# A list scheduler's view of PSUM banks and of weight loads, in a one-core hybrid diffusion step

## The chip, the core and the metric

The kernel runs on one core of one Trainium2 chip. Its time is the device time of one execution in microseconds (us); the median of three runs is the metric. The engines are TensorE (PE in the profile, with its weight loads as PEld), VectorE (DVE), ScalarE (ACT), GpSimd (POOL) and SyncE (SP), which issues the DMA transfers.

## The reference

One inference step of a two-layer hybrid backbone (DEPTH is 2) over 128 prompt tokens and 512 latent tokens, in fp32, with D_MODEL 1024 and D_FF 2816. Cut to what matters:

```python
def _token_mixer(h, lw, ctx):
    (z, xbc, dt_raw, rq, rk, rv, rg, aq, ak, av, mcq, mckv) = jnp.split(h @ lw['w_in'], split_at, axis=-1)
    xbc = jax.nn.silu(_dwconv_centred(xbc, lw['ssd_conv_w'], lw['ssd_conv_b']))
    ...
    y, ssd_f, ssd_b = _bidir_scan(ch, bh * dt[:, :, 0, :, None], ...)          # SSD, 8 heads
    o_ssd = _rmsnorm(y.reshape(bsz, L, SSD_INNER) * jax.nn.silu(z), lw['ssd_norm_w'])
    o, ret_f, ret_b = _bidir_scan(rq, rk, rk, rv, la_f, la_b, ...)             # retention, 4 heads
    o_ret = (_head_layernorm(o)... * lw['ret_gn_w'] * jax.nn.silu(rg))
    o_att = _attention(q_att, keys, vals, ATT_HEAD_DIM ** -0.5)...             # grouped-query, 8 heads
    o_mla = _attention(q_m, k_m, v_m, (MLA_NOPE + MLA_ROPE) ** -0.5)...        # latent attention, 8 heads
    g = jax.nn.sigmoid((h @ lw['w_merge'] + lw['b_merge']).astype(f32))
    merged = (g[:, :, 0] * (o_ssd @ lw['w_br_ssd']) + g[:, :, 1] * (o_ret @ lw['w_br_ret'])
              + g[:, :, 2] * (o_att @ lw['w_br_att']) + g[:, :, 3] * (o_mla @ lw['w_br_mla']))
    return merged @ lw['w_out'], cache

def _trunk_layer(x, mod, lw, ctx):      # mod = silu(cond) @ w_mod + b_mod
    h = _rmsnorm(x, lw['g_pre_mix']) * (1.0 + sc_a) + sh_a
    x = x + g_a * _rmsnorm(_token_mixer(h, lw, ctx), lw['g_post_mix'])
    h = _rmsnorm(x, lw['g_pre_ffn']) * (1.0 + sc_f) + sh_f
    return x + g_f * _rmsnorm(_conv_ffn(h, lw), lw['g_post_ffn'])
```

## The kernel before

**Products.** Activations lie feature-major, 128 features by 640 tokens a tile, in two halves of 320 tokens. Every linear layer takes each weight as a high part and a low part, and each activation likewise (`ah0` to `ah7` and `al0` to `al7` are the eight tiles of the normed input). One 128x128 weight block and one half of the tokens make three matmuls of 320 columns into a PSUM bank `lin`: high weight by `ah`, high weight by `al`, low weight by `ah`. The weights come in blocks of 512 columns: `weights()` has SP load `wr` (256 KB), ACT copy it to `wh` (the high part), and DVE subtract to `wl` (the low part, called the split below). There are four buffers of `wr`, three of `wh` and three of `wl`.

**Order.** The kernel's Python doesn't issue instructions. A `Recorder` keeps every operation, finds which depend on which, ranks them and lays down one fixed list per engine; the engines then run their lists strictly from the top. All instructions so carry one line, L603. `depend()` compares the regions that two operations touch: an operation waits in the plan only for those with an overlapping region. A matmul's rank is its due time on PE, in ns, in the order of recording; that of any other operation is that time plus 20,000 (`LATE`), then lowered where something that needs it ranks lower. `order()` steps through time with estimated durations and takes, on each engine, the operation of lowest rank whose inputs are ready and whose buffer is free. Work recorded for the next modulation (loads `wm`, DVE operations `wj`) is ranked 300,000 behind and fills idle time. The plan sees parts of a bank; the semaphores that the finished program carries are set for the whole tile, a bank.

**Where banks are shared.** PSUM has eight banks: four `lin`, three `st`, one `pv`. In the retention branch several products go to one `st` bank and are read piece by piece: the value transposes in `ret_in` (four or two 128x128 products, each copied by ACT to another tile `K`), and `values` and `out` of `ret`:

```python
            for h in range(4):
                self.mm(p[:, hs[h]], o[:, hs[h]], dg[:, hs[h]])
            for h in range(4):
                self.stt(z[:, hs[h]], p[:, hs[h]], self.P("gnw", h), z[:, hs[h]])
```

**Order of the stages in a layer.** Modulation and norm; input products of the SSD branch, its convolution, its softplus (`dt`) and its eight heads (`st` and `pv` products of `m` tiles that DVE and ACT make, four pieces of work to a head); with them the products for `z`; retention; merge of branch 0; attention; latent attention with the other merges; the last merge and the output product, then the FFN. Layer 1 begins near 1470 us.

Of the kernel before, what the change touches and what calls it, by code (L numbers as in the profile page):

```python
# [214 lines left out]
CST = CC["distF"][0]  # L215
MB = 10
BEHIND = 300e3
FFN_ORDER = (2, 1, 0, 3, 4, (0, 4), 5, 6, 7, 8, (4, 8), 9, 10, 11, 12, (8, 12), 13, 14, 15, 16, (12, 16), 17, 18, 19, 20, 21)
FFN_LAST = (16, 22)
RST, RHD = (2, 2), (4, 2)  # L220
# [64 lines left out]
class View:  # L285
# [36 lines left out]
    def region(self):  # L322
        a, b = int(self.ix.flat[0]), int(self.ix.flat[-1])
        if self.h.dram:
            return 0, 0, a, b
        n = self.h.n
        return a // n, b // n, a % n, b % n


# [40 lines left out]
SLACK, LOAD, LATE = 250.0, 109.0, 20e3  # L370
# [3 lines left out]
class Recorder:  # L374
# [64 lines left out]
    def depend(self):  # L439
        for o in self.ops:  # L440
            o.preds, o.succs, o.new, o.tiles = set(), [], [], []
            seen = set()
            for w, vs in ((False, o.reads), (True, o.writes)):
                for v in vs:
                    h = v.h
                    if h.ro:
                        continue
                    if id(h) not in seen:
                        seen.add(id(h))
                        if h.tag is not None:  # L450
                            o.tiles.append(h)
                            h.left += 1
                            o.new.append(h)
                            if w and o.eng == "tensor":
                                if h.pe is not None:
                                    o.preds.add(h.pe)
                                h.pe = o
                    p0, p1, a, b = v.region()
                    keep = []
                    for e in h.acc:  # L460
                        q, ew, s0, s1, c, d = e
                        if (w or ew) and q is not o and s0 <= p1 and p0 <= s1 and c <= b and a <= d:
                            o.preds.add(q)
                            if w and p0 <= s0 and s1 <= p1 and a <= c and d <= b:
                                continue
                        keep.append(e)
                    keep.append((o, w, p0, p1, a, b))
                    h.acc = keep
            if o.gate is not None:
                o.preds.add(o.gate)  # L470
            for q in o.preds:
                q.succs.append(o)
        t = 0.0
        for o in self.ops:
            o.cost = self.cost(o)
            o.prio = t if o.eng == "tensor" else t + o.bias + LATE
            if o.eng == "tensor":
                t += max(o.cost[0], LOAD)
        for o in reversed(self.ops):
            for q in o.preds:  # L480
                if q is not o.gate:
                    w = q.cost[1] + LAT[q.eng] + (DMA_NS if q.eng == "sync" else 0.0) if q.eng != o.eng else q.cost[0]
                    q.prio = min(q.prio, o.prio - w)

    def order(self):
        from heapq import heappush, heappop
# [7 lines left out]
        slots = {t: [0.0] * self.bufs[t] for t in self.count}  # L494
# [9 lines left out]
        def blocked(o, t):  # L504

            for h in o.new:
                if id(h) in made:
                    continue
                g = h.tag
                need = h.seq - low[g] - sum(1 for k in ahead[g] if k < h.seq) + 1  # L510
                if len(slots[g]) < need:
                    return g, None
                w = sorted(slots[g])[need - 1]
                if w > t:
                    return g, w
            return None

        while len(done) < len(self.ops):
            best = None
            for e in engs:  # L520
                t = free[e]
# [5 lines left out]
                elif pending[e]:  # L527
                    t, _, i = pending[e][0]
# [3 lines left out]
                if lock > t and self.ops[i].cost[2]:  # L532
                    t = lock
# [3 lines left out]
            t, asked, e = best  # L537
# [4 lines left out]
            p, i = heappop(avail[e])  # L542
            o = self.ops[i]
            b = blocked(o, t) if o.new else None
            if b:
                if b[1] is None:
# [4 lines left out]
            for h in o.new:  # L551
                if id(h) not in made:
                    made.add(id(h))
                    g = h.tag
# [10 lines left out]
            if e == "tensor":  # L565
                t = max(t, loaded + LOAD)
# [17 lines left out]
            for h in o.tiles:  # L584
                h.left -= 1
                h.end = max(h.end, o.end + LAT[e])
                if not h.left:
                    g = h.tag
# [20 lines left out]
class Net:  # L609
# [102 lines left out]


    def weights(self, src, n, eng=None):
        r = self.sbt(512, "wr", WR)
        h = self.sbt(512, "wh", WB, F32R)
        lo = self.sbt(512, "wl", WL, F32R)
        self.load(r[:, :n], src)
        self.act(h[:, :n], r[:, :n])
        self.tt(lo[:, :n], r[:, :n], h[:, :n], ALU.subtract, eng=eng or self.nc.vector)  # L720
        return h, lo

    def lin_fm(self, src, kt, xh, xl, m=128, unit=4, halves=((0, 320), (320, 640))):
# [210 lines left out]
    def mod_units(self, l, blocks, halves, tile, pool=()):  # L934
# [3 lines left out]
        for hv in halves:  # L938
# [10 lines left out]
            for j in blocks:  # L949
                for hf in hv:  # L950
                    self.rec.bias = BEHIND
                    w = self.sbt(512, "wm", 2)
                    self.load(w[:, :512], self.A["wmod"][l, j][:, hf * 512 : hf * 512 + 512])
                    for q in range(2):
# [11 lines left out]
                        yield  # L966
                        self.rec.bias = BEHIND
            self.rec.bias = 0
# [1125 lines left out]
    def ffn(self, l, x, Gf, hh, hl):  # L2094
# [40 lines left out]

        for f in FFN_ORDER:
            if isinstance(f, tuple):
# [54 lines left out]
```

## Time and profile before

| what | value |
|---|---|
| runs | 2990.85, 2990.12, 2987.82 us; median 2990.12 us |
| the profiled execution | 2992.41 us, of which the span is 2990.4 us |
| mean granted TensorE clock | 0.985 |
| PE, PEld, DVE, ACT, POOL busy | 96%, 90%, 72%, 47%, 3% of the span |
| chain that ended last | PE 66%, DVE 6%, issue 2%, DMA 2%, ACT 2% |
| DMA | 329.67 MB, mean 110 GB/s |

Busy time is the time in which an engine has an instruction under way; matmuls overlap each other. The granted clock is the share of full speed that the chip gave TensorE. A wait is idle time of an engine ahead of an instruction, named by the instruction that ended it.

### The profile page before, as it was taken

What the parts mean: (1) busy time and instruction counts of PE and PEld (TensorE: products, weight loads), DVE (VectorE), ACT (ScalarE), POOL (GpSimd) and SP (SyncE); (2) the same over time, 40 slices, a digit from 0 to 9 for tenths busy, and PEclk for the clock granted to TensorE, in tenths of its full rate; (3) what the DMA queues carried; (4) which work ended last, traced back from release to release, by engine and by line L of the source; (5) the groups of instructions that cost most, each with busy time, mean ns of one, the idle gap of its engine ahead of it and who ended that gap; (6) DMA issues with size and microseconds to landing.
All of it is one profiled execution on the core that took longest, in us unless ns stands there. A gap on an engine that the chain in (4) does not pass through costs nothing.

```text
span 2990.4 us, 50157 instructions
## 1 busy us (share of the span) xinstructions
PE 2884.4 (96%) x18638; PEld 2693.3 (90%) x18638; DVE 2156.5 (72%) x4548; ACT 1395.1 (47%) x3013; POOL 79.6 (3%) x99
## 2 busy tenths in 40 slices
PE   8999999999998999999997999999999999999998
PEld 5789998897898999999985998988978999999997
DVE  5885748747888899888888743387478577666667
ACT  4434337547734643333454342375476455433333
POOL 0000010000000000000000000100000000000000
PEclk9999999999998999999997999999999999999999
DMA  5124430134365444444331232211342443222223
GB/s 216 45 89 140 158 109 34 63 108 141 100 215 173 154 137 148 133 140 131 107 128 38 86 120 80 86 34 63 108 134 86 139 134 132 88 75 75 78 74 110
DMA packets 193412, 329.67 MB, mean 110 GB/s; under 512 B 20880, under 2 KB 54288, under 8 KB 193168
## 3 DMA queue, kind: packets, MB, share of 16 engines
q1 hardware_dynamic: 193168, 326.46, 33.4%
q8 instruction: 147, 2.41, 0.3%
q14 instruction: 97, 0.79, 0.1%
HBM read 293.41 MB, written 32.96 MB: 109 GB/s over the span
## 4 chain that ended last, share of the span: by engine, by line
PE 66%; DVE 6%; issue 2%; DMA 2%; ACT 2%; SPq 0%; POOLq 0%; POOL 0%; DVEq 0%; ACTq 0%
PE lin L603 55%; PE st L603 7%; PE pv L603 4%; DVE m L603 3%; DVE wl L603 1%; DVE X L603 1%; DMA wm<-in_wmod 1%; ACT m L603 0%; DVE al L603 0%; DVE wj L603 0%; DMA g<-od 0%; DMA vd<-g 0%; ACT K L603 0%; ACT wh L603 0%; ACT Q L603 0%
## 5 line engine op out<-in xcount | busy, mean ns | idle before, releaser
L603 PE MATMUL lin<-ah,wh 128*128 128x320 f32 (+1 forms) x3776 | 1159.5, 314 | 2.8 <-ACT wh L603 1.3
L603 PE MATMUL lin<-al,wh 128*128 128x320 f32 (+1 forms) x3776 | 1149.3, 311 | 8.4 <-DVE al L603 8.1
L603 ACT ACTIVATE wh<-wr 128x512 fp32r<-128x512 f32 (+2 forms) x796 | 490.7, 617 | 1100.6 <-PE lin L603 772.8
L603 PE MATMUL lin<-ah,wl 128*128 128x320 f32 x3744 | 944.2, 311 | 17.3 <-DVE wl L603 17.3
L603 DVE TENSOR_TENSOR wl<-wr,wh 128x512 fp32r<-128x512 f32 (+2 forms) x790 | 530.6, 673 | 356.5 <-ACT wh L603 344.4
L603 PEld LDWEIGHTS lin<-al,wh 128*128 128x128 f32 (+1 forms) x3776 | 709.7, 188 | 18.8 <-DVE al L603 13.0
L603 PEld LDWEIGHTS lin<-ah,wh 128*128 128x128 f32 (+1 forms) x3776 | 711.4, 189 | 15.0 <-issue 6.5
L603 PEld LDWEIGHTS lin<-ah,wl 128*128 128x128 f32 x3744 | 650.5, 189 | 25.5 <-DVE wl L603 19.7
L603 PE MATMUL lin<-K,wh 128*128 128x320 f32 (+1 forms) x1472 | 293.3, 312 | 1.8 <-ACT K L603 1.4
L603 DVE TENSOR_TENSOR m<-m,m 128x512 fp32r<-128x512 f32 (+6 forms) x393 | 245.8, 632 | 49.6 <-ACT m L603 43.1
L603 ACT ACTIVATE m<-st 128x512 fp32r<-128x512 f32 (+3 forms) x480 | 220.3, 524 | 107.7 <-PE st L603 99.7
L603 PEld LDWEIGHTS lin<-K,wh 128*128 128x128 f32 x1472 | 237.7, 189 | 3.6 <-ACT K L603 2.0
L603 DVE SCALAR_TENSOR_TENSOR wj<-wm,silc 128x512 bf16<-128x512 f32 x320 | 219.9, 687 | 27.2 <-DMA wm<-in_wmod 23.4
L603 PE MATMUL lin<-O,wh 128*128 128x320 f32 x1024 | 217.0, 314 | 5.2 <-ACT g L603 4.0
L603 PE MATMUL pv<-m,K 128*128 128x512 f32 (+2 forms) x832 | 216.2, 355 | 2.6 <-issue 0.7
L603 PE MATMUL lin<-K,wl 128*128 128x320 f32 (+1 forms) x736 | 185.5, 313 | 4.5 <-DVE wl L603 4.5
L603 PEld LDWEIGHTS lin<-O,wh 128*128 128x128 f32 x1024 | 168.6, 190 | 11.4 <-ACT g L603 4.5
L603 PEld LDWEIGHTS pv<-m,K 128*64 128x64 f32 (+1 forms) x832 | 120.5, 165 | 28.6 <-issue 9.7
L603 PE MATMUL st<-Q,K 128*128 128x512 f32 (+3 forms) x480 | 136.2, 384 | 0.6 <-ACT Q L603 0.3
L603 PE MATMUL lin<-O,wl 128*128 128x320 f32 x512 | 133.0, 313 | 3.4 <-DVE wl L603 3.4
L603 PEld LDWEIGHTS lin<-K,wl 128*128 128x128 f32 x736 | 128.6, 189 | 5.9 <-DVE wl L603 5.9
L603 POOL TENSOR_TENSOR rq<-rq,mhalf 128x3 f32<-128x3 f32 (+3 forms) x41 | 58.1, 1416 | 2628.5 <-DVE rq L603 2535.2
(195 smaller groups left out, 3045.5 us busy)
## 6 DMA issues: line engine op xcount, KB each, us to landing
wr<-in_wup SPq DMA_DIRECT2D x196, 256.0 KB, 2.6
wr<-in_wmg SPq DMA_DIRECT2D x160, 256.0 KB, 2.7
wm<-in_wmod SPq DMA_DIRECT2D x160, 256.0 KB, 2.9
wr<-in_win SPq DMA_DIRECT2D x142, 256.0 KB, 2.6
wr<-in_wdn SPq DMA_DIRECT2D x94, 256.0 KB, 2.6
wr<-in_wbr SPq DMA_DIRECT2D x80, 256.0 KB, 2.7
wr<-in_wout SPq DMA_DIRECT2D x64, 256.0 KB, 2.8
g<-od SPq DMA_DIRECT2D x32, 320.0 KB, 4.0
```

Of the source, the lines that this page charges most:

```text
L603: f(*[_plain(v) for v in o.args], **{k: _plain(v) for k, v in o.kw.items()})
```

## The change

Three edits of the planner. A region in PSUM is the whole bank, so that two operations on one bank depend on each other wherever they touch it, in the order of recording. The three operations of `weights()` get a bias of -60,000: it is left out of the first ranking and added after the ranks were lowered, so that load, copy and split of a weight block rank 60 us ahead of what they would have had (the buffers still limit how far they go). And a matmul that takes a PSUM buffer is planned 250 ns (`SLACK`) behind the time at which the buffer comes free. No instruction is added or removed.

```diff
+AHEAD = -60e3
...
         n = self.h.n
+        if self.h.tag[0] == "ps":
+            return 0, 127, 0, n - 1
         return a // n, b // n, a % n, b % n
...
-            o.prio = t if o.eng == "tensor" else t + o.bias + LATE
+            o.prio = t if o.eng == "tensor" else t + max(o.bias, 0) + LATE
...
                     q.prio = min(q.prio, o.prio - w)
+        for o in self.ops:
+            o.prio += min(o.bias, 0)
...
-                w = sorted(slots[g])[need - 1]
+                w = sorted(slots[g])[need - 1] + (SLACK if o.eng == "tensor" else 0.0)
...
     def weights(self, src, n, eng=None):
+        self.rec.bias = AHEAD
...
+        self.rec.bias = 0
         return h, lo
```

Of PE's 17,810 instructions 13,494 keep their place. 282 of 790 splits stand earlier on DVE (by up to 143 places), 169 of 796 copies on ACT, 167 of 793 weight loads on SP (by up to 36). The FFN stretches are as before.

The first place is a value transpose of the retention in layer 0, on PE, between input products (`lin`) of the next tile; `g` holds the values, `cst` the matrix. Before, four products in a row go to one bank, each with a wait for ACT:

```order
L603 MATMUL lin_419_2171<-ah0_18_292,wl_423_2099 128x320 [waits DVE_49]
L603 MATMUL st_416_2181<-cst_1_100,g_407_2169 128x128 [waits Activation_49] x4
L603 MATMUL st_417_2194<-cst_1_100,g_407_2169 128x128 x2
L603 MATMUL lin_420_2175<-ah0_18_292,wl_423_2099 128x320
L603 MATMUL lin_419_2171<-ah1_19_299,wh_422_2085 128x320
```

In the changed kernel two of them wait, and input products stand between:

```order
L608 MATMUL lin_419_2133<-ah0_18_294,wl_423_2065 128x320 [waits DVE_49]
L608 MATMUL st_416_2144<-cst_1_111,g_407_2131 128x128 [waits Activation_49]
L608 MATMUL st_417_2150<-cst_1_111,g_407_2131 128x128 x2
L608 MATMUL lin_420_2140<-ah0_18_294,wl_423_2065 128x320
L608 MATMUL lin_419_2133<-ah1_19_302,wh_422_2047 128x320
L608 MATMUL st_416_2144<-cst_1_111,g_407_2131 128x128 [waits Activation_49]
L608 MATMUL st_416_2144<-cst_1_111,g_407_2131 128x128 x2
L608 MATMUL lin_419_2133<-al1_27_318,wh_422_2047 128x320
```

Over the whole program, matmuls of transposes with a wait for ACT go from 36 to 20, those of `values` from 20 to 6, and those of `out` with a wait for DVE from 21 to 10: 41 fewer. In the attention 26 score products get a wait for PE itself, where 31 `pv` products had one.

The second place is DVE in the SSD branch of layer 1, where the convolution (`m<-K,hc`, `X<-m,m`) and the softplus (`m_3882`) run. `wl_4041` and `wl_4044` are the splits for the first `z` product. Before, they stand behind both:

```order
L603 SCALAR_TENSOR_TENSOR X_3919_18093<-m_3920_18085,m_3918_18075 128x641
L603 SCALAR_TENSOR_TENSOR m_3882_18050<-m_3882_18050 128x80
L603 TENSOR_TENSOR wl_4041_18096<-wr_4039_17906,wh_4040_17995 128x512
L603 SCALAR_TENSOR_TENSOR m_3882_18050<-m_3882_18050 128x80
L603 TENSOR_TENSOR wl_4044_18101<-wr_4042_17928,wh_4043_18014 128x512
```

In the changed kernel they stand 25 places higher in the list, among the convolution's first operations and ahead of the last input products' evacuation (`m_3756`, `K_3757`):

```order
L608 TENSOR_SCALAR m_3915_18001<-K_3761_17715,hc_3583_16709 128x641
L608 TENSOR_TENSOR wl_4041_18007<-wr_4039_17906,wh_4040_17995 128x512
L608 SCALAR_TENSOR_TENSOR m_3895_17969<-K_3758_17503,hc_3583_16709,m_3895_17969 128x641
L608 TENSOR_TENSOR wl_4044_18024<-wr_4042_17928,wh_4043_18012 128x512
L608 TENSOR_TENSOR m_3756_17455<-m_3756_17455,lin_3877_17973 48x320
L608 TENSOR_SCALAR K_3757_17471<-lin_3867_17947 128x1
```

The third place is the end of the SSD heads in layer 1, on PE: `st_4016<-m_4028` is the first product of the last head. Before, 211 input products stand between the end of the SSD's own input products (`lin_3877`) and it, and a third output of `z` is under way:

```order
L603 MATMUL lin_4064_18768<-ah5_3591_17365,wl_4071_18724 128x320
L603 MATMUL lin_4065_18777<-ah5_3591_17365,wl_4071_18724 128x320
L603 MATMUL lin_4064_18768<-ah6_3592_17374,wh_4070_18653 128x320
L603 MATMUL lin_4064_18768<-al6_3600_17387,wh_4070_18653 128x320
L603 MATMUL st_4016_18805<-m_4028_18759,K_3922_18208 64x128
```

In the changed kernel there are 423, and the retention's outputs are under way:

```order
L608 MATMUL lin_4124_19152<-ah1_3587_17286,wh_4126_19030 128x320
L608 MATMUL lin_4124_19152<-al1_3595_17331,wh_4126_19030 128x320
L608 MATMUL st_4016_19091<-m_4028_19073,K_3922_18326 64x128
L608 MATMUL lin_4123_19149<-ah1_3587_17286,wl_4127_19120 128x320
L608 MATMUL lin_4124_19152<-ah1_3587_17286,wl_4127_19120 128x320
```

On DVE the operation that reads the last head's bank stands 22 places later in its list, 9 of them splits. In layer 0 the same product has 83 more input products ahead of it, and DVE's operation 10 more places, 4 of them splits.

At the start of the program SP's list before begins with the modulation weights `K<-in_wmod` and the input `c2t`; four loads of `wr` stand at the 33rd to the 48th place. In the changed kernel three of these stand first of all and the fourth ahead of the eighth modulation weight; on DVE the first split stands ahead of `c2s`, the operation that PE's first matmul needs, and on ACT the first copy likewise.

## Rows read from the trace of the kernel before

**Rows 1.** The page: span, and busy time of PE.

```profile
span 2990.4 us, 50157 instructions
PE 2884.4 (96%) x18638; PEld 2693.3 (90%) x18638; DVE 2156.5 (72%) x4548; ACT 1395.1 (47%) x3013; POOL 79.6 (3%) x99
```

**Rows 2.** Waits of PE, whole span: total us, times, longest us.

```profile
PE lin L603 <- DVE wl L603: 25.2, 16, 9.9
PE st L603 <- DVE m L603: 13.1, 9, 3.2
PE st L603 <- ACT K L603: 8.2, 20, 0.7
PE lin L603 <- DVE al L603: 8.1, 8, 2.9
```

**Rows 3.** Waits of PE at 215:248, at 270:350 (two rows), and at 1770:1850.

```profile
PE st L603 <- ACT K L603: 2.9, 8, 0.4
...
PE st L603 <- ACT m L603: 3.3, 7, 0.5
PE st L603 <- DVE g L603: 1.8, 4, 0.4
...
PE st L603 <- DVE g L603: 3.1, 7, 0.4
```

**Rows 4.** Timeline at 216 us: start, busy, engine, operation, [idle before <- releaser].

```profile
216.16 0.61 PE L603 MATMUL st<-cst,g 128*128 128x128 f32 x4
...
217.14 0.49 PE L603 MATMUL st<-cst,g 128*128 128x128 f32 x2 [0.37 <-ACT K L603]
...
217.66 0.28 ACT L603 ACTIVATE K<-st 128x128 f32<-128x128 f32 x1 [0.58 <-PE st L603]
...
217.99 0.82 PE L603 MATMUL st<-cst,g 128*128 128x128 f32 x5 [0.37 <-ACT K L603]
...
218.57 0.39 PE L603 MATMUL lin<-ah,wl 128*128 128x320 f32 x1
```

**Rows 5.** Timeline of PE, of DVE and of ACT, SSD branch of layer 1.

```profile
1570.67 0.31 PE L603 MATMUL lin<-al,wh 128*128 128x320 f32 x1
1580.89 0.90 PE L603 MATMUL lin<-ah,wl 128*128 128x320 f32 x2 [9.92 <-DVE wl L603]
...
1580.15 0.68 DVE L603 TENSOR_TENSOR wl<-wr,wh 128x512 fp32r<-128x512 f32 x1
...
1569.45 0.62 ACT L603 ACTIVATE wh<-wr 128x512 fp32r<-128x512 f32 x1
```

**Rows 6.** Windows: length, busy time (instructions) of PE, PEld, DVE, ACT, POOL; clock, DMA share, GB/s.

```profile
57.00:100.00 43.00, 43.00 (x293) 42.38 (x292) 31.12 (x64) 18.36 (x40) 0.00 (x0) 1.00 0.26 83
1568.20:1600.00 31.80, 19.84 (x127) 16.29 (x127) 23.96 (x53) 16.64 (x35) 0.00 (x0) 0.79 0.13 44
1600.00:1668.50 68.50, 60.15 (x303) 43.63 (x304) 61.05 (x166) 23.52 (x45) 0.00 (x0) 0.88 0.10 35
100.00:184.00 84.00, 78.57 (x446) 58.91 (x445) 73.78 (x189) 35.18 (x72) 0.00 (x0) 0.96 0.14 47
880.00:930.00 50.00, 40.33 (x225) 38.51 (x224) 42.39 (x113) 20.40 (x38) 0.00 (x0) 0.83 0.58 188
0.00:25.00 25.00, 16.95 (x44) 3.80 (x45) 6.47 (x12) 8.26 (x14) 0.37 (x5) 1.00 0.94 337
270.00:350.00 80.00, 74.84 (x520) 70.85 (x519) 56.15 (x150) 28.87 (x85) 8.74 (x14) 0.98 0.54 172
1695.00:1750.00 55.00, 52.07 (x358) 50.52 (x357) 16.44 (x30) 20.32 (x55) 1.17 (x1) 1.00 0.19 63
```

**Rows 7.** Timeline of PE: the last wait for a load at the start.

```profile
20.43 1.02 PE L603 MATMUL lin<-K,c2s 128*2 128x512 f32 x2 [1.18 <-DMA K<-in_wmod]
```

**Rows 8.** The page, groups of instructions: busy us, mean ns, idle before and its main releaser.

```profile
L603 DVE TENSOR_TENSOR wl<-wr,wh 128x512 fp32r<-128x512 f32 (+2 forms) x790 | 530.6, 673 | 356.5 <-ACT wh L603 344.4
...
L603 PE MATMUL pv<-m,K 128*128 128x512 f32 (+2 forms) x832 | 216.2, 355 | 2.6 <-issue 0.7
```

## The prediction

> **What bounds the kernel now.** Read the page first: PE is busy for 2884.4 of 2990.4 us [rows 1], so that at most some 100 us can be won from its idle time, and what else there is to win lies in stretches at a lower granted clock. The waits of PE come next, since they say whom it waits for. The largest group is the splits, 25.2 us in 16 waits, one of 9.9 us; DVE's `m` tiles of the SSD heads cost 13.1 us, and ACT's `K` tiles 8.2 us in 20 short waits [rows 2]. The windows show where these lie. In the SSD branch of layer 1 (1568.2 to 1668.5 us) PE is busy for 19.84 of 31.8 and 60.15 of 68.5 us, at clocks of 0.79 and 0.88; DVE is busy for 23.96 and 61.05 us there [rows 6]. Length less busy time times clock gives what PE loses: 31.8 - 15.7 = 16.1 us and 68.5 - 52.9 = 15.6 us. The same sum gives 8.6 us for layer 0's SSD branch (100 to 184) and 16.5 us for the last merge of layer 0 (880 to 930) [rows 6]. Beside these, a stretch of plain products loses nothing: 293 matmuls in 43.00 us, 0.147 us each [rows 6].
>
> **The bank waits.** In the retention PE, having put one product into an `st` bank, waits until the reader of that piece is through before it puts in the next. Rows 4 show it: PE resumes 0.37 us after it stopped, ACT then waits 0.58 us for the new product, and so on. From 216.16 to 218.57 us there are 11 products; the last five, unhindered, start 0.58 / 5 = 0.116 us apart, so the 11 would take 1.28 us, and the two waits cost 2.41 - 1.28 = 1.13 us, 0.57 us each [rows 4]. There are eight such waits in the value transposes of each layer, 7 and 4 in `values` and `out` of layer 0, 7 and 7 in layer 1, 41 in all, with 2.9 + 3.3 + 1.8 + 2.9 + 3.3 + 3.1 = 17.3 us of idle time [rows 3], where layer 1's transposes and its `values` show the same 2.9 and 3.3 as layer 0's. With the whole bank as one region, the pieces are read when all are written, and the order counts 41 waits fewer; where two remain (a transpose that needs the second half of its tile) input products stand between. PE has such products to do meanwhile: in layer 1's transposes DVE is busy for 16.44 of 55 us and nothing else holds PE [rows 6]. The gain is 41 x 0.57 = 23 us; it can't be more than that by much, and it would be some 10 us if the readers, which now start later, hold up what follows them.
>
> [...] These stretches have a granted clock of 0.98 and 1.00 [rows 6], full speed but for 0.02 x 74.84 = 1.5 us in each of two. [...]
>
> **The splits in layer 1's SSD branch.** PE stops at 1570.67 us plus its last matmul and goes on at 1580.89 us, having waited 9.92 us for a split [rows 5]. The copy that the split needs was made at 1569.45 + 0.62 = 1570.07 us, and the split itself takes 0.68 us, at 1580.15 [rows 5]: for ten microseconds it stood behind convolution and softplus in DVE's list. In the changed list it stands ahead of most of these, so PE gets it near 1571. What is late instead is the convolution, by two splits, and with it the heads, for which PE waits already (13.1 us in both layers [rows 2]). So the wait as such isn't the gain; the gain is what PE gets done in the meantime. At the last head's first product PE has 212 more input products behind it, 212 x 0.147 = 31 us of work that no longer has to be done afterwards, when PE is the bound (52.07 of 55 us busy, clock 1.00 [rows 6]). Against it DVE has 22 more operations to do before that head is read: 9 splits of 0.673 us [rows 8] and 13 others at the stretch's mean of 61.05 / 166 = 0.37 us [rows 6], 11 us. If DVE's idle time stays, the heads end 11 us later, and the gain is 31 - 11 = 20 us. DVE is idle for 7.8 + 7.5 = 15.3 us of the two windows [rows 6]; if all 11 us went into that, the gain would be 31. If the moved products run at the low clock of 0.88 or below and delay the heads' own, it is down to 10. I take 20, since DVE's idle time is mostly a chain (Fc, Wc, the head's tiles) that more work doesn't shorten.
>
> **Layer 0's SSD branch**, by the same reckoning: 83 input products, 12 us, against 4 splits at 0.673 and 6 others at 73.78 / 189 = 0.39 us, 5 us; gain 7 us (4 to 9, since PE loses only 8.6 us there).
>
> **The last merge and the other splits.** Between 880 and 930 us PE loses 16.5 us; the modulation's DVE operations now stand behind the merge's own, so that the `g` buffers come free sooner. I take a third, 5 us (2 to 9). Outside the SSD branch 25.2 - 9.9 = 15.3 us of waits for splits are left in 15 waits [rows 2], at the ends of norms. Some vanish there, but in the output products of both layers the splits that went ahead now delay the last `al` tiles, for which PE waits 8.1 us already [rows 2]. I take a third to a half of 15.3, less 1.5 us for the `al` tiles: 5.5 us (0 to 12).
>
> **What it costs.** At the start the loads are the bound: in the first 25 us the DMA share is 0.94 at 337 GB/s [rows 6], and PE waits for a modulation weight as late as 20.43 us [rows 7]. Four loads of 256 KB now go ahead of these: 1.05 MB / 337 GB/s = 3.1 us. Nothing hides it, since the next products need those very loads. Also PE's first operation stands behind a load, a copy and a split, but the same transfers hold it anyway. Cost 3 us (2 to 5). The 26 score products that get a wait for PE itself: 31 `pv` products have one now, and all 832 of them have 2.6 us of idle time [rows 8], under 0.1 us for each of the 31; 2 us (0 to 3). Loads of modulation weights that are later by 5 to 23 places are ranked far behind their use; nothing.
>
> **Sum.** 23 + 20 + 7 + 5 + 5.5 - 3 - 2 = 55.5 us off the profiled execution's 2992.4 us: 2936.9. The median of the runs is 2.3 us below that execution, so 2934.6, rounded to 2935 us.
>
> **Rivals.**
> (a) Only the bank waits go. For it speaks that DVE is busy for 61.05 of 68.5 us in the heads [rows 6]: if DVE and not PE bounds the SSD branch, each split put ahead pushes the heads back by what it gave PE. Then 23 - 3 - 2 = 18 us are won: 2972 us. Against it: 31 us of PE's work move for 11 us of DVE's.
> (b) More than forecast: SSD gains 31 and 9, the merge 9, the other splits 12, and the clock follows. 23 + 31 + 9 + 9 + 12 - 5 = 79 us: 2911 us.
> (c) Slower: splits at the head of DVE's list that aren't ready. DVE is idle for 344.4 us before splits, waiting for ACT's copies, 344.4 / 790 = 0.44 us each [rows 8]. Of the 282 that moved ahead each may now hold up, for that long, operations that PE waits for. If all did, 282 x 0.44 = 124 us would be lost, and the time would be 2990 - 55 + 124 = 3059 us; at 55.5 / 0.44 = 126 of them, under half, the gain is gone, and at 140 the kernel is slower by 6 us. Against it: copies and loads went ahead as well, in the same order, and where DVE waits most for a copy, in the plain products, no other work stands behind that split.
> (d) The bank waits only change place: readers start later, and the products that need them wait as long. Then 2935 + 23 = 2958 us at most; the `lin` products between them speak against it.
>
> [...]
>
> **How the numbers follow.** Chances: forecast with its own range (2918 to 2952) 0.55, (a) 0.15, (b) 0.12, (d) 0.10, (c) 0.05, no change 0.03, which would be the sum of half of (c) and the gain. A range of 2908 to 2968 us leaves out (c), no change, most of (a) beyond 2968 and the far part of (b), 0.2 together. Under 0.2%, 6 us, is about what a measurement of this kernel can't tell from no change. Faster 0.92, same 0.03, slower 0.05.
>
> **What would show it.** Right: in the stretches of rows 3, no group of short waits `st` for ACT `K` or DVE `g`; no wait of 9.9 us near 1570; SSD windows at a clock above 0.9 with more matmuls in them; the stretch after the last head shorter by 20 us net. First modulation wait that ends near 23 us in place of 20.4. Wrong: waits of `st` for DVE `m` that grow by 20 us or more in the SSD branch (then (a)); DVE's idle time before splits well above 344 us together with more waits of PE for `al` and `m` (then (c)); waits of `lin` or `st` for `K` and `g` of the old size at other places (then (d)).

## The result and the profile after

The changed kernel takes 2919.22 us (median of four runs, 2915.53 to 2924.92) against 2990.48 us (2987.82 to 2996.48): a ratio of 0.9761, 95% interval 0.9739 to 0.9783, 71 us or 2.4% less. The prediction was 2935 us, in a range of 2908 to 2968.

The page of the changed kernel's profiled execution (2915.53 us), as in [rows 1]:

```profile
span 2913.4 us, 50176 instructions
PE 2849.6 (98%) x18638; PEld 2683.4 (92%) x18638; DVE 2151.2 (74%) x4548; ACT 1390.3 (48%) x3013; POOL 79.0 (3%) x99
```

The waits of PE over its whole span (total us, times, longest us), as in [rows 2]:

```profile
PE lin L608 <- DVE c2s L608: 8.0, 1, 8.0
PE lin L608 <- ACT K L608: 7.5, 5, 4.5
PE st L608 <- DVE m L608: 7.5, 6, 2.3
PE lin L608 <- DVE al L608: 7.5, 9, 2.0
PE lin L608 <- DVE O L608: 4.7, 2, 4.3
...
PE lin L608 <- DVE wl L608: 1.3, 5, 0.3
```

The splits have fallen from 25.2 us to 1.3, and `st` for ACT's `K` and `m` is off the list. Grown are `lin` for ACT's `K` (from 1.4 us to 7.5, one wait of 4.5) and for DVE's `O` (from 0.4 to 4.7, one of 4.3), and the wait at the start is 8.0 us long, not 4.4. PE's busy time is 35 us less for the same matmuls; the mean granted clock went from 0.985 to 0.993.

Where the time went is best seen by following the same matmuls in both traces. Wherever PE has issued the same set of instructions in both lists, the start of the next one is read in each, and the difference is taken from stage to stage (us; stages in the time of the kernel before; negative is a gain). Small stages are left out. The other columns belong to the experiments below.

```
stage                           change   bank   bias  250ns  bank+   bias   maxima  norms,
                                         only   only   only   bias    -10   togeth. maxima
   0-  97 start                    0.9   -0.9    0.9   -0.8    0.5   -1.0    -0.5    -1.3
  97- 199 SSD, layer 0            -7.8    0.5   -0.8    0.1   -1.1   -6.7    -0.3    -7.8
 199- 350 retention, layer 0     -10.9  -12.0   -2.6   -0.1   -8.6   -8.9    -1.5   -10.3
 440- 835 attentions, layer 0     -7.2   -1.0    0.2   -7.9    3.1   -5.6    -1.2    -8.9
 835-1045 merges, output         -13.9   -1.4  -12.6   -2.1  -13.6   -8.1    -2.5    -9.8
1045-1468 FFN                      3.1    0.0    3.2    0.0    3.3    3.1     0.2     0.0
1468-1555 change of layer          5.3    0.8    4.2   -0.5    2.5    4.1     0.7     0.8
1555-1705 SSD, layer 1           -20.8   -2.5  -15.1   -0.4  -12.4    0.9     3.4   -20.7
1705-1845 retention, layer 1     -16.6  -16.8    0.4    0.0  -15.7  -16.8    -1.5   -16.6
1950-2320 attentions, layer 1     -8.3    0.0    1.3   -6.8   -0.2   -6.5    -3.7    -8.7
2320-2973 merges, output, FFN     -0.5    0.2    2.2    0.0   -0.3   -1.1    -0.1    -1.0
sum                              -76.8  -33.1  -18.7  -18.9  -42.6  -46.8    -7.0   -84.8
```

One execution scatters within such a stage: a second profile of the changed kernel had 3.2 at the change of layer, and layer 1's SSD branch with one and the same PE order gave -14.8 and -20.7, in the two runs below with the bias off ahead of the norms. Their windows of that branch, as in [rows 6], differ in the granted clock, 0.94 and 0.99:

```profile
1516.90:1652.20 135.30, 131.50 (x771) 109.98 (x770) 113.88 (x270) 57.34 (x113) 1.47 (x2) 0.94 0.24 75
1517.60:1647.10 129.50, 125.72 (x772) 105.31 (x771) 113.61 (x270) 57.44 (x113) 1.46 (x2) 0.99 0.25 79
```

Differences of 2 to 3 us in the table, and up to 6 in the SSD rows, prove nothing alone.

The windows of the change of layer, the SSD branch and the retention (two windows), first before, then after, each pair with the same work of PE:

```profile
1468.00:1555.00 87.00, 78.27 (x484) 74.42 (x483) 70.89 (x178) 46.32 (x106) 5.84 (x7) 0.90 0.42 134
1555.00:1705.00 150.00, 129.69 (x770) 108.89 (x770) 129.15 (x312) 62.28 (x127) 1.47 (x2) 0.90 0.21 68
...
1705.00:1752.00 47.00, 44.07 (x305) 42.52 (x304) 11.40 (x23) 17.33 (x49) 1.17 (x1) 1.00 0.18 58
1752.00:1845.00 93.00, 86.56 (x606) 82.31 (x605) 47.13 (x111) 36.36 (x98) 8.03 (x14) 0.98 0.38 121
```

```profile
1432.40:1524.50 92.10, 81.15 (x483) 78.82 (x482) 70.67 (x175) 46.39 (x105) 5.50 (x7) 0.87 0.43 127
1524.50:1653.90 129.40, 125.61 (x771) 104.87 (x770) 113.81 (x270) 57.44 (x113) 1.51 (x2) 0.99 0.25 78
...
1653.90:1696.00 42.10, 42.10 (x304) 42.05 (x304) 26.39 (x66) 22.10 (x63) 1.17 (x1) 1.00 0.21 68
1696.00:1775.30 79.30, 79.30 (x592) 77.72 (x591) 45.58 (x110) 33.95 (x95) 8.03 (x14) 1.00 0.45 142
```

Four things are to be seen. In the retention PE is busy from end to end, where it was idle for 2.9 and 6.4 us. In the SSD branch the same 770 matmuls meet 114 us of DVE's work and not 129: 15 us of it now fall into the retention (11.40 to 26.39 in the window behind), where DVE had room. And the clock in that branch is 0.99, not 0.90. At the change of layer things are worse: five microseconds longer at a lower clock.

### The profile page after: what moved, and what is told of

The parts are those of the page before. It is cut to its first block, busy times and chain, and to the rows that moved or that the text cites. A ratio compares the mean times of both kernels' runs of the same rounds, so it can differ in the third digit from the quotient of the medians.

```text
span 2913.4 us, 50176 instructions
## 1 busy us (share of the span) xinstructions
PE 2849.6 (98%) x18638; PEld 2683.4 (92%) x18638; DVE 2151.2 (74%) x4548; ACT 1390.3 (48%) x3013; POOL 79.0 (3%) x99
## 3 DMA queue, kind: packets, MB, share of 16 engines
q8 instruction: 147, 2.41, 0.3%
## 4 chain that ended last, share of the span: by engine, by line
PE 86%; DVE 6%; DMA 3%; issue 2%; ACT 1%; SPq 0%; POOL 0%; DVEq 0%; POOLq 0%; ACTq 0%
PE lin L608 70%; PE st L608 11%; PE pv L608 5%; DVE m L608 2%; DVE wl L608 1%; DMA wm<-in_wmod 1%; DVE wj L608 1%; DVE X L608 1%; DMA K<-in_wmod 0%; ACT K L608 0%; DVE al L608 0%; DMA vd<-g 0%; DVE K L608 0%; ACT m L608 0%; DVE g L608 0%
## 5 line engine op out<-in xcount | busy, mean ns | idle before, releaser
L608 PEld LDWEIGHTS lin<-al,wh 128*128 128x128 f32 (+1 forms) x3776 | 708.1, 188 | 19.9 <-DVE al L608 11.4
L608 PE MATMUL pv<-m,K 128*128 128x512 f32 (+2 forms) x832 | 204.6, 344 | 0.9 <-ACT m L608 0.5
L608 DVE TENSOR_REDUCE nm<-st 128x1 f32<-128x320 f32 (+1 forms) x288 | 122.7, 461 | 7.3 <-PE st L608 5.8
```

The lines of the kernel that those rows point to most:

```text
L608: f(*[_plain(v) for v in o.args], **{k: _plain(v) for k, v in o.kw.items()})
```

## The experiments

**The three edits, each alone, and two together.** The bank edit alone is the two new lines of `region()`; the bias alone is `AHEAD` with its three uses; the 250 ns alone is `SLACK` on a buffer; the fourth kernel is the change without this last one:

```diff
-                w = sorted(slots[g])[need - 1] + (SLACK if o.eng == "tensor" else 0.0)
+                w = sorted(slots[g])[need - 1]
```

> The region of a PSUM view is the whole bank; no bias for the weights, no SLACK on buffers. In its order 41 waits of the retention are gone and DVE's list is the old one but for 7 in 100 rows. Theory 1, the bank edit gives the retention's gain alone (0.57 us for each of 41 waits, 23 us; the changed kernel's trace shows 27 us there): 2963 to 2967 us against 2990. Rival, the bank edit also gives the 16 us that the attention stretches won in the changed kernel: 2947 us. Rival (d) of the prediction, the waits only change place: 2985 us or more.

> The bias of -60 us for load, copy and split alone. Its order has 181 more input products ahead of the last SSD head of layer 1 (212 in the whole change) and 32 in layer 0 (83). Theory 1: the SSD branches give 18 + 3 us, the last merge 9, the change of layer costs 5 and the start 1: some 24 us, 2966 us. Rival, the attention's 16 us come from loads and splits that stand earlier there: 2950 us. Rival, without the bank edit the moved splits only push the heads: 2985 us or more.

> Only the 250 ns on a matmul that takes a PSUM buffer. In its order 12 of 18 interruptions of the attention's transposes of maxima are gone, 26 score products wait for PE itself, and 38 and 24 more input products stand ahead of the last SSD head of layer 1 and 0. Theory 1: this is where the attention's 16 us come from, with some 4 us of the SSD branches: 2970 to 2974 us. Rival, the edit does nothing by itself (the prediction gave it a cost of 2 us): 2988 to 2994 us.

> The whole change but for the 250 ns on a buffer. Theory 1: 2919 us plus the attention's 16 and a few of layer 0's SSD branch, 2935 to 2940 us. Rival, the 250 ns do nothing: 2919 us.

Measured beside 2993.14 us of the kernel before: the bank edit 2965.78 us (ratio 0.9899, 0.9883 to 0.9916), the bias 2973.51 (0.9930, 0.9913 to 0.9948), the 250 ns 2977.45 (0.9941, 0.9925 to 0.9956), bank edit and bias 2949.54 (0.9848, 0.9827 to 0.9870). The bank edit's gain lies in the retention (-12.0 and -16.8 in the table) and nowhere else beyond the scatter: theory 1, and rival (d) of the prediction falls. In the run of the bank edit alone the transposes of one block show it, beside [rows 4]:

```profile
215.80 1.39 PE L608 MATMUL st<-cst,g 128*128 128x128 f32 x11
...
216.89 1.13 ACT L608 ACTIVATE K<-st 128x128 f32<-128x128 f32 x6 [0.64 <-PE st L608]
...
216.94 0.39 PE L608 MATMUL lin<-ah,wl 128*128 128x320 f32 x1
```

The eleven records (six transposes, two records each, of which one is missing; the prediction counts them as products) take 1.14 us up to the next `lin` product, none of them waited for, and ACT reads all six pieces at once behind them; before, the same eleven took 2.41 us.

The 250 ns were given no gain in the prediction, only a cost of 2 us; alone they give 16 us, nearly all of it in the attentions (-7.9 and -6.8) and none in the SSD branches (0.1 and -0.4), where some 4 us were expected. Without them the change has a ratio of 0.9848 in place of 0.9761, some 26 us, 5 to 10 more than expected: the attentions lose 18 us in the traces, and layer 0's SSD branch loses 7. That branch gains in the whole change (-7.8), but not with the bias, the 250 ns or bank edit and bias (-0.8, 0.1, -1.1); bank edit and 250 ns without the bias were not run, so whether it takes the bias isn't shown. The bias alone gives the last merge and layer 1's SSD branch (-12.6, of which the FFN takes 3.2 back, and -15.1), and costs 4.2 at the change of layer; its run is 20 us below the kernel before, where theory 1 had 24, with nothing won in the attentions (0.2 and 1.3).

**A smaller bias,** `AHEAD = -10e3`, the rest of the change as it is.

> The whole change with a bias of -10 us in place of -60. In its order the two splits for the first z product are back behind convolution and softplus, and only 38 more input products (212) stand ahead of the last head of layer 1, 50 (83) of layer 0. Theory 1, the SSD gain is in proportion: layer 1 gives 4 of 20 us, layer 0 some 4 of 8, the change of layer no longer costs 5: 2933 to 2937 us. Rival, the SSD gain comes from elsewhere (bank edit, 250 ns): 2915 to 2920 us.

2944.25 us beside 2990.94 (0.9846, 0.9833 to 0.9860), above both expected numbers. In the waits of PE from 1500 to 1650 us the old wait is back, to the tenth, and another stays:

```profile
PE lin L608 <- DVE wl L608: 9.9, 1, 9.9
...
PE lin L608 <- ACT K L608: 4.5, 1, 4.5
```

All of layer 1's SSD gain is gone (0.9 in the table; 4 us were expected to stay), with bank edit and 250 ns in place: it comes from splits that stand far enough ahead. The change of layer still loses 4.1 us, against the expectation: for that a bias of 10 us is enough.

**The bias off ahead of the norms.** Weights of the FFN and of the SSD branch's input products keep the old rank:

```diff
+        self.ahead = True
...
     def weights(self, src, n, eng=None):
-        self.rec.bias = AHEAD
+        self.rec.bias = AHEAD if self.ahead else 0
...
+        self.ahead = False
         self.lins(specs, 0 if l else 7)
+        self.ahead = True
...
     def ffn(self, l, x, Gf, hh, hl):
+        self.ahead = False
```

> The whole change, but the weights of the FFN and of the SSD branch's input products keep the old rank; from the z products on the bias is there as before. The order up to the last SSD heads' place is that of the change in count. Theory 1, splits ahead of the norm cost the 5.3 us at the change of layer, and the loads ahead 0.9 us at the start: 2912 to 2914 us. Rival, the loss there comes from the bank edit or the 250 ns, or the norm takes it anyway: 2919 us.

2911.77 us beside 2990.94 (0.9739, 0.9725 to 0.9753), as expected; its interval meets the changed kernel's, so this run alone doesn't settle it. The loss at the change of layer is gone from the trace (0.2 us, not 5.3), and that the bias makes it is shown by the bias alone, too. How it comes about stands in the changed kernel's timeline:

```profile
1458.44 0.41 DVE L608 TENSOR_TENSOR wl<-wr,wh 128x256 fp32r<-128x256 f32 x1
...
1459.51 0.68 DVE L608 TENSOR_TENSOR wl<-wr,wh 128x512 fp32r<-128x512 f32 x1
...
1461.57 0.47 DVE L608 TENSOR_TENSOR O<-O,lin 128x320 f32<-128x320 f32 x1
...
1462.19 0.87 PE L608 MATMUL lin<-K,wh 128*128 128x320 f32 x2 [4.25 <-DVE O L608]
...
1501.85 1.04 ACT L608 ACTIVATE K<-lin 128x128 f32<-128x128 f32 x4
1502.18 0.54 PE L608 MATMUL lin<-ah,wh 128*128 128x320 f32 x1 [4.51 <-ACT K L608]
```

With its splits ready, PE goes on until it needs a `lin` bank that hasn't been read, and waits for the reader. The reader (`O<-O,lin` on DVE, `K<-lin` on ACT) stands behind the norm's chain, and that chain now has the splits among it. The wait for a split has become a longer wait for a bank. Before, PE waited 2.48 and 0.95 us for splits there; with the bias off, it waits for 2.43 and 1.06.

**Which buffers the 250 ns act on.** The kernel before, with the 250 ns for one tag of PSUM tile each:

```diff
-                w = sorted(slots[g])[need - 1]
+                w = sorted(slots[g])[need - 1] + (SLACK if o.eng == "tensor" and g == ("ps", "st") else 0.0)
```

> The kernel before with the 250 ns for buffers of the tag st alone. The 26 waits for PE itself are in its order; 5 of 18 interruptions of the transposes of maxima are gone. Theory 1, st buffers (three, which scores, transposes and maxima share) are where the attention's gain comes from: all but some 2 us of the 16 that the edit won alone, 2975 to 2979 us. Rival, it comes from pv: 2988 us or more.

> The kernel before with the 250 ns for the single pv buffer alone; 8 of 18 interruptions are gone, no wait for PE itself is added. Theory 1, gain only by the interruptions, 8 x 0.44 = 3.5 us: 2986 to 2990 us. Rival, pv is where the attention's gain comes from: 2975 to 2979 us.

2984.16 (0.9977, 0.9968 to 0.9986) and 2984.17 us (0.9978, 0.9968 to 0.9987) beside 2990.94, 7 us each. No theory's number was met: neither tag alone is where the 16 us come from, each brings nearly half. In the four stretches of the attention heads (440 to 580, 700 to 835, 1950 to 2110, 2170 to 2320) the traces have 5.0 us less with `st`, 4.0 with `pv` and 11.4 with both. The interruptions of the maxima's transposes that are gone (5 of 18, 8 of 18; 12 with both) don't go in step with these gains; the next run prices them.

**The interruptions.** In the trace of before the five transposes of a head's maxima (`nm`; four go to one bank, the fifth to another, and each leaves two records) are broken up by `pv` products:

```profile
486.00 0.60 PE L603 MATMUL st<-cst,nm 128*1 128x128 f32 x4
486.74 0.50 PE L603 MATMUL pv<-m,K 128*128 128x128 f32 x3
487.17 0.81 PE L603 MATMUL st<-cst,nm 128*1 128x128 f32 x6
487.92 0.50 PE L603 MATMUL st<-Q,K 128*128 128x512 f32 x1
488.25 0.31 PE L603 MATMUL lin<-O,wh 128*128 128x320 f32 x1
```

and in that of the change they are together:

```profile
467.47 1.25 PE L608 MATMUL st<-cst,nm 128*1 128x128 f32 x10
468.66 0.50 PE L608 MATMUL pv<-m,K 128*128 128x128 f32 x3
469.00 0.45 PE L608 MATMUL st<-Q,K 128*128 128x512 f32 x1
469.28 0.45 PE L608 MATMUL lin<-O,wh 128*128 128x320 f32 x2
```

From the first transpose to the `lin` product that is 2.25 us and 1.81, 0.44 us less, and PE counts as busy nearly all the time in both (2.10 us of the 2.25, and all of the 1.81). The experiment gives the transposes a rank 3 us earlier in the kernel before, and nothing else:

```diff
-        o.bias, o.gate = self.bias, self.gate
+        o.bias, o.gate, o.early = self.bias, self.gate, 0.0
...
+        for o in self.ops:
+            o.prio -= o.early
...
-                self.mm(p[r0 : r0 + 1, i * 128 : (i + 1) * 128], nm[:, i : i + 1], self.C("ident"))
+                self.mm(p[r0 : r0 + 1, i * 128 : (i + 1) * 128], nm[:, i : i + 1], self.C("ident")).early = 3000
```

> The kernel before; only the five transposes of a head's maxima rank 3 us earlier, so that nothing is put between them. The 18 interruptions are gone, the rest of the order is the same in count. Theory 1, the interruptions are what the 250 ns save in the attention (over the runs so far some 1 us for each that is gone): 14 to 18 us, 2973 to 2977 us. Rival, an interruption costs the 0.44 us that one block shows: 8 us, 2983 us. Second rival, they only come along with it: 2990 us.

2987.91 us beside 2993.58 (0.9982, 0.9970 to 0.9994), 1.8 to 9.0 us by the interval. Theory 1 falls, and so does the second rival: a price near that of the one block holds. In the four stretches of the heads the trace has 6.5 us less. The 18 count the interruptions among the four transposes of one bank, 6.5 / 18 = 0.36 us for each; but the run also closes six between the fourth and the fifth transpose (24 in the trace of before, none in this one), and over all of them it is 6.5 / 24 = 0.27 us. By either count the 250 ns take away 12, worth 3 to 4 of the 11.4 us that these stretches gain by them.

**A kernel that beats both.** The change once more; the change with the bias off ahead of the norms and the transposes together; and that with 400 ns in place of 250.

> The changed kernel once more, on the same chip as the others of this call: 2916 to 2922 us.

> The whole change, with the bias off for the weights of the FFN and of the SSD branch's input products, and the transposes of maxima together (0 interruptions in place of 3). Theory 1: 2 to 7 us below the changed kernel for the norms and 3 for the maxima, 2909 to 2913 us. Rival: within the scatter of the changed kernel, 2916 to 2922 us.

> As the one before, with 400 ns in place of 250 on a buffer: 20 more input products ahead of the last head of layer 0, the same in layer 1. Theory 1, these are worth what DVE doesn't need for them, 1 to 2 us in layer 0: 2907 to 2912 us. Rival, later buffers cost more than that in the attention: 2913 us or more.

Beside 2993.58 us the change took 2920.48 us (2915.09 to 2924.51; 0.9754, 0.9735 to 0.9773), the second 2907.57 us (2906.58 to 2913.83; 0.9716, 0.9699 to 0.9734), the third 2914.78 us (2910.14 to 2918.58; 0.9732, 0.9715 to 0.9749). The second is 13 us below the change on the same chip, and their runs don't overlap: better than expected by a little. In its table column start and change of layer have lost their price. What the transposes add to the bias off ahead of the norms isn't clear of the scatter (0.9739 without them, and the intervals meet). Nor is it shown that 400 ns cost more than 250, since those intervals meet too; layer 0's SSD branch, which was to gain, gained 4.2 us and not 7.8.

## Why the prediction was right, and where it was not

**The bank waits** were forecast at 23 us and gave 27 by the run of the edit alone, 27 to 29 by the stages. The mechanism, place and count were right. The clock had a part: the stretch that was at 0.98 is at 1.00 now, by an estimate from the clocks 0.02 x 86.56 = 1.7 us of the 13.7 that it became shorter. Before, the clock was 0.50 for 3.40 us right behind three waits of `values` (rows of the timeline, then a window); `lin` products in that window start 0.27 us apart (1818.38, 1818.64, 1818.91 us), where plain products take 0.147 us each at a clock of 1.00 [rows 6]:

```profile
1814.93 0.71 PE L603 MATMUL st<-K,m 128*128 128x128 f32 x4 [0.54 <-ACT m L603]
1816.10 0.71 PE L603 MATMUL st<-K,m 128*128 128x128 f32 x4 [0.46 <-ACT m L603]
1817.27 0.78 PE L603 MATMUL st<-K,m 128*128 128x128 f32 x2 [0.46 <-ACT m L603]
...
1817.30:1820.70 3.40, 3.40 (x13) 3.40 (x14) 0.17 (x1) 0.85 (x3) 1.75 (x2) 0.50 0.13 40
```

Layer 0's stretch, at 0.98 before [rows 6], has 1.00 in the run of the bank edit alone (270:340) and in the changed kernel (247:332). The forecast's 23 us have no term for the clock; by the same estimate that was some 3 us too little (1.5 in layer 0, 1.7 in layer 1), as far as runs of this scatter can tell. That the waits make the clock drop isn't shown: at 1695:1750, with eight short waits of PE for ACT's `K`, 2.9 us in all, it was 1.00 [rows 6].

**Layer 1's SSD branch** was forecast at 20 us and gave 20.8. The step held that the wait itself isn't the gain, and the windows bear it out: DVE's work was moved into the retention, PE's ahead of it. The heads ended later, as reckoned: their last `st` product of `m` began 115.2 us after the start of the branch's window before (1670.24) and 124.0 after it now (1648.49), 8.7 us later where 11 were expected. The run with a bias of 10 us shows the cause. What the step's sum didn't name is the clock: of the 20.6 us by which the window is shorter, 13.7 are, by an estimate from the clocks, what a clock below full speed no longer takes (0.10 x 150.00 before, less 0.01 x 129.40 now). That the size came out within 1 us is luck, since the same order gave 14.8 in another run. And 5.3 us of it only make up for the change of layer just ahead; the net is 15.

**Layer 0's SSD branch** was forecast at 7 us and gave 7.8, from a reason that was half right at most: it takes the 250 ns as well, since neither the bias nor the bias with the bank edit brings it.

**The last merge** was forecast at 5 us and gave 9.5 (880 to 945 us); the bias alone shows the same 9.3. The term was sized at a third of what PE loses there, a choice; more than half came back, with the clock at 0.97 where it was 0.87 from 880 to 945. Its reason holds in outline: PE's waits for ACT's `g` there, 4.0 us before, are gone, and 37 of the modulation's `wj` operations on DVE fall into the window in place of 44, though they still stand among the merge's own.

**The other splits** were forecast at a gain of 5.5 us; they were a loss of 4 (-4.3 and 3.1 behind the merge, 5.3 at the change of layer, -0.5 behind layer 1's attentions). The waits for splits did vanish. The step that failed is that a third to a half of them would be won: it asked what is late next only for the `al` tiles, not for the readers of the `lin` banks, which stood in DVE's and ACT's lists behind the same chain.

**The start** was forecast at a loss of 3 us. PE's first matmul came 3.6 us later (7.99, not 4.40) and the last wait for a load ended 2.3 us later:

```profile
7.99 8.35 PE L608 MATMUL lin<-K,c2s 128*2 128x512 f32 x16 [7.99 <-DVE c2s L608]
...
22.70 1.88 PE L608 MATMUL lin<-K,c2s 128*2 128x512 f32 x4 [1.26 <-DMA K<-in_wmod]
```

At 52 us 0.9 of it was left. "Nothing hides it" was wrong in part; that the blocks loaded early are not loaded later is the likely reason, which no run tested.

**The 26 waits for PE itself** were booked as a cost of 2 us. The edit that brings them won 15 us in the attentions. The prediction named what it adds to the order and not what it takes away, though the interruptions, a part of it, could be counted in both lists. This is the largest error, 17 us, and most of what the kernel was faster than forecast (16 us by the medians, 21 by the profiled executions); the other errors nearly cancel.

**The rivals.** (a), that DVE bounds the SSD branch and only the bank waits are won, fell with the stage's 20.8 us. (b), more than forecast, came nearer by its number (2911 us) than the forecast did, but not by its reason: it had 31, 9 and 12 us for the SSD branches and the other splits, where 20.8, 7.8 and a loss of 4 came, and nothing for the attentions. The forecast's own range held, at its end, by errors that partly cancel. (c), splits that aren't ready, didn't come: DVE's idle time before splits fell, beside [rows 8]:

```profile
L608 DVE TENSOR_TENSOR wl<-wr,wh 128x512 fp32r<-128x512 f32 (+2 forms) x790 | 530.0, 672 | 307.2 <-ACT wh L608 297.0
```

What stays open: 7 to 8 of the 11 us that the heads gain by the 250 ns alone. They come with fewer changes of PE between `pv` and `st` products: in the traces, around the heads, 423 before, 348 and 401 with the 250 ns for `st` and for `pv` alone, 334 with both. With the transposes of the maxima together there are 424, so that their 6.5 us came without this. Neither buffer alone brings the whole, and no run changed that number by itself; it goes along with the gain and isn't shown to be its cause.

## What to carry to other kernels

When a planner decides the order, count in both lists what every edit moves, the smallest too: a tolerance of 250 ns was worth 16 us alone, where the bank edit was worth 27. Tell a planner what the program will wait for (here a bank), or it will put into the order waits that it can't see. A prefetch ahead of everything was right where its engine had room behind (20.8 us won; DVE was busy for 11.40 of the 47.00 us behind), and wrong where the same engine must empty the buffers that the faster engine fills (5.3 us lost, with a wait of 4.25 us for DVE's `O`); look for the reader of the buffers before ranking anything ahead of it.

## What was not expected of the hardware

Ten records of short products (five transposes) in a row start 0.12 us apart, but breaking the row once costs 0.44 us in the one block and 0.27 to 0.36 us as a mean over the heads, with PE shown as busy nearly throughout (2.10 of 2.25 us in that block): the busy share alone does not show it, the same work followed in two traces does. And the granted clock differs from stage to stage: in layer 1's SSD branch it went from 0.90 to 0.99, while PE's idle time fell from 20.3 us to 3.8, and at the change of layer from 0.90 to 0.87, where that grew from 8.7 us to 10.95. But with one and the same order it was 0.94 in one run of that branch and 0.99 in another, 5.8 us apart, with PE idle for 3.8 us in both: what sets it isn't shown.
